# Recurrent mixer: the factors towards a chunk's end, made on ScalarE from those towards its beginning

## The chip, the cores and the metric

The kernel runs on one core of a Trainium2 chip, in one launch. The metric is device time in microseconds (us). The kernel before takes 2109.54 us, the median of three runs between 2107.28 and 2109.99.

## The reference, cut to what matters

The reference is a network of two layers over 512 tokens: 256 of context and 256 of the sequence proper. Each layer has a modulated norm, one input projection, three mixers side by side (neighbourhood attention with 8 heads, a recurrent mixer of the RWKV-7 kind with 4 heads of 64, and an mLSTM with 4 heads), an output projection, and a mixture of 32 experts of which each token takes two. The change is in the recurrent mixer alone:

```python
def rwkv7_scan(r, w, k, v, a, b, S0, emit):
    def step(S, inp):
        r_t, w_t, k_t, v_t, a_t, b_t = inp
        sa = jnp.einsum('bhvk,bhk->bhv', S, a_t)
        S = S * w_t[:, :, None, :] + sa[..., None] * b_t[:, :, None, :] + v_t[..., None] * k_t[:, :, None, :]
        return S, (jnp.einsum('bhvk,bhk->bhv', S, r_t) if emit else None)
...
    log_w = -jax.nn.softplus(-(w0 + jnp.einsum('blzr,zrc->blzc', wd, w2))) - 0.5
    decay = jnp.exp(-jnp.exp(log_w))
    a = jax.nn.sigmoid(a0 + jnp.einsum('blzr,zrc->blzc', ad, a2))
...
    k_dir = k[:, :, None] * (1.0 + (a - 1.0) * k_a)
    b_dir = kk.reshape(B, L, 1, RW_WIDTH) * a
```

It runs forward and backward (d = 0, 1). Since decay = exp(-kappa * s), with s a sigmoid and kappa = exp(-0.5), the product of decays over some steps is the exponential of a sum of s.

## The kernel before

Time is cut into 8 chunks of 64 steps, and the scan becomes products of small matrices: factors are applied to r, k, kk and b, so that what happens inside a chunk is matmuls, and only the state goes from chunk to chunk. The 256 columns are two halves (ct = 0, 1) of 128 partitions. So a layer has four items (d, ct), and a tile of 128x512 holds one item's 512 steps, each chunk 64 columns of it.

For each item `rw_feat` (line 645) makes the features. Two small matmuls and `sigm` (three activations) give S, the sigmoid s of the decay, and A, the a of the reference. A scan on VectorE (line 663) sums S inside each chunk: `cum`. From it come `tot` (the chunk's total), `Xx` = cum - S, and `Yy` = tot - cum. By direction these play three roles: `incl`, the sum up to a step with it; `excl`, the sum without it; `rem`, what remains to the chunk's end. ScalarE takes exponentials: `En` = exp(kappa * incl), and exp(-kappa * .) of incl, excl, rem and tot (`gc`). Then T gets -kk * excl and r * incl; `b` = kk * a; `kd` = k * (1 + (a - 1) * k_a), as a tensor_scalar on A and a product with k. BK holds b and kd times En: these stand in the matmuls inside the chunk (lines 697 to 704), whose masked results Aa go out to memory for the inverse (`rw_inv16`) and stay as MA. BH holds b and kd times rem: it is transposed (lines 717 to 721) and stands in the update of the state, in MA's first block. Line 725 copies a part of T over BK.

The two-tensor products go through the helper `tt` of line 649, so the profile shows them all on that line and tells them apart by tile: SA holds S and A, cX holds cum and Xx, and Yk holds Yy and kd. `CFG['fG']` chooses the engine of four of them. In layer 0 it is 0, and Xx, b and the two products of BH run on GpSimd; in layer 1 it is 1, and Xx runs on VectorE and the other three on GpSimd.

`rwkv` runs rw_feat of the next item, then `rw_mid`, `rw_inv16` of the next and `rw_seq` of this one. Beside them run the projections of the other mixers (`ml_proj`, `na_proj`), as filler for TensorE; their weights are split into a high and a low part, the high one on ScalarE (lines 472, 999), the low one on VectorE or GpSimd (lines 475, 1000). The program is written with a tile framework: a planner orders each engine's instructions by priority (offsets per function, in `CHOICES`) and by its own estimates of when operands are ready. Each engine then works in that fixed order and waits where an operand is late. BK and BH come from a pool of 15 pages, T, MA, Aa, SA, cX and Yk too.

After the mixers follow attention and mLSTM items with the output projection (`cores`), the routing, and the experts, whose weights stream from memory.

Of the kernel before, what the change touches and what calls it, by code (L numbers as in the profile page):

```python
# [14 lines left out]
AF = mybir.ActivationFunctionType  # L15
ALU = mybir.AluOpType
# [5 lines left out]
S = 256  # L22
# [5 lines left out]
KAPPA = float(np.exp(np.float32(-0.5)))  # L28
# [118 lines left out]
CFG = dict(CHOICES)  # L147
# [66 lines left out]
class K:  # L214
# [427 lines left out]
    def c8(self, t):  # L642
        return t.rearrange("p (c s) -> p c s", s=64)

    def rw_feat(self, d, ct, st):

        nc = self.nc
        V, G, A_ = nc.vector, nc.gpsimd, nc.scalar
        tt = lambda e, o, x, y, op: e.tensor_tensor(o, x, y, op)
        c8 = self.c8  # L650
        bc = lambda t: t.unsqueeze(2).to_broadcast([t.shape[0], t.shape[1], 64])
        sl = slice(ct * 512, (ct + 1) * 512)
        R, Kx, KK = self.Rf[:, sl], self.Kf[:, sl], self.KK[:, sl]
# [3 lines left out]
        S, A = self.w2("SA")  # L657
# [3 lines left out]
        self.sigm(A, ps, bias=self.nwa[:, 4 + j:5 + j], scale=-1.0)  # L661
        cum, Xx = self.w2("cX")
        V.tensor_tensor_scan(cum, self.rst, S, 0.0, ALU.mult, ALU.add)
        Yy, kd = self.w2("Yk")
        tot = self.sm([8], "tot")
        V.tensor_copy(tot, c8(cum)[:, :, 63])
        tt(V if CFG['fG'] & 1 else G, Xx, cum, S, ALU.subtract)
        tt(V, c8(Yy), bc(tot), c8(cum), ALU.subtract)
        if d == 0:
            incl, excl, rem = cum, Xx, Yy  # L670
        else:
            incl, excl, rem = S, Yy, Xx
            tt(V, S, S, Yy, ALU.add)
        T = st["T"] = self.w("T")
        tv = T.rearrange("p (c b s) -> p c b s", b=2, s=64)
        gc = st["gc"] = self.sm([8], f"gc{ct}", bufs=2)
# [2 lines left out]
        A_.activation(En, incl, AF.Exp, scale=KAPPA)  # L679
        A_.activation(excl, excl, AF.Exp, scale=-KAPPA)  # L680
        A_.activation(incl, incl, AF.Exp, scale=-KAPPA)
        A_.activation(rem, rem, AF.Exp, scale=-KAPPA)
        V.scalar_tensor_tensor(tv[:, :, 0, :], c8(KK), -1.0, c8(excl), ALU.mult, ALU.mult)
        tt(V, tv[:, :, 1, :], c8(R), c8(incl), ALU.mult)
        b = A
        V.tensor_scalar(kd, A, self.pr[:, 26 + ct:27 + ct], self.oka[:, ct:ct + 1], ALU.mult, ALU.add)
        tt(V if CFG['fG'] & 2 else G, b, KK, A, ALU.mult)
        tt(V, kd, kd, Kx, ALU.mult)
        BK, BH = self.w("BK"), self.w("BH")
        v4 = lambda t: t.rearrange("p (i b s) -> p i b s", b=4, s=64)  # L690
        i4 = lambda t: t.rearrange("p (i b s) -> p i b s", b=2, s=64)
        tt(V, v4(BK)[:, :, 0:4:3, :], i4(b), i4(En), ALU.mult)
        tt(V, v4(BK)[:, :, 1:3, :], i4(kd), i4(En), ALU.mult)
        tt(V if CFG['fG'] & 4 else G, v4(BH)[:, :, 0:4:3, :], i4(b), i4(rem), ALU.mult)
        tt(V if CFG['fG'] & 8 else G, v4(BH)[:, :, 1:3, :], i4(kd), i4(rem), ALU.mult)
        MA = st["MA"] = [self.w("MA"), self.w("MA")]
        Aa = st["Aa"] = self.w2("Aa")
        mk = self.c("maskA")[:, d * 128:(d + 1) * 128]
# [1 line left out]
        for g in range(2):  # L700
            pa = [self.pf(), self.pf()]
            for ci in range(4):
                c = g * 4 + ci
# [13 lines left out]
        for g in range(2):  # L717
            pt = self.pf()
            for ci in range(4):
                c = g * 4 + ci  # L720
# [12 lines left out]
        for pr in range(4):  # L733
            for hh in range(2):
                for par in range(2):
                    c = 2 * pr + par
# [1260 lines left out]
```

## Time and profile before

| | us |
|---|---|
| median of 3 runs | 2109.54 |
| profiled execution | 2105.22 |
| its span, first to last instruction | 2103.4 |
| TensorE busy (matmul) | 1835.3 |
| VectorE busy | 992.4 |
| ScalarE busy | 475.0 |
| GpSimd busy | 460.0 |

The profile is of one execution. Its slices show the recurrent mixer of layer 0 from about 95 to 350 us and that of layer 1 from about 1190 to 1440 us; from 600 to 1100 and from 1600 on the DMA engines are busy nearly all the time with expert weights. A busy time of TensorE says that matmuls were under way, not that it was at its peak. A wait is put down to the releaser that came last.

### The profile page before, as it was taken

What the parts mean: (1) busy time and instruction counts of PE and PEld (TensorE: products, weight loads), DVE (VectorE), ACT (ScalarE), POOL (GpSimd) and SP (SyncE); (2) the same over time, 40 slices, a digit from 0 to 9 for tenths busy, and PEclk for the clock granted to TensorE, in tenths of its full rate; (3) what the DMA queues carried; (4) which work ended last, traced back from release to release, by engine and by line L of the source; (5) the groups of instructions that cost most, each with busy time, mean ns of one, the idle gap of its engine ahead of it and who ended that gap; (6) DMA issues with size and microseconds to landing.
All of it is one profiled execution on the core that took longest, in us unless ns stands there. A gap on an engine that the chain in (4) does not pass through costs nothing. (4 is left out here: it accounts for less than half of the span.)

```text
span 2103.4 us, 29644 instructions
## 1 busy us (share of the span) xinstructions
PE 1835.3 (87%) x11375; PEld 952.4 (45%) x11379; DVE 992.4 (47%) x2079; ACT 475.0 (23%) x993; POOL 460.0 (22%) x338
## 2 busy tenths in 40 slices
PE   7989889989998899899995879899999888987985
PEld 3767666545443243224434667675443231323221
DVE  3687563467732334334447585653464122322223
ACT  2643222425210000000114542212331000000000
POOL 1232122234401112111125342231141001100001
PEclk9998999879999999999997888897799999999997
DMA  8332232751769998999992222244756969999995
GB/s 284 126 79 56 60 61 81 304 204 61 264 276 384 409 371 339 392 408 393 389 388 78 70 69 62 59 108 185 266 207 278 405 265 418 416 416 416 415 418 228
DMA packets 192881, 531.33 MB, mean 253 GB/s; under 512 B 77520, under 2 KB 107632, under 8 KB 155232
## 3 DMA queue, kind: packets, MB, share of 16 engines
q1 hardware_dynamic: 190656, 524.76, 65.9%
q0 software_dynamic: 928, 2.50, 0.4%
q8 instruction: 92, 1.51, 0.3%
q10 hardware_dynamic: 1152, 2.13, 0.3%
q14 instruction: 53, 0.43, 0.1%
HBM read 521.87 MB, written 7.47 MB: 252 GB/s over the span
## 5 line engine op out<-in xcount | busy, mean ns | idle before, releaser
L282 PE MATMUL ps<-rg,xe 128*32 128x512 f32 (+2 forms) x2280 | 484.2, 619 | 49.4 <-DMA rg<-in_exp_w_up_dram 29.8
L282 PE MATMUL pe<-rg,HT 128*32 128x512 f32 (+2 forms) x1120 | 233.8, 645 | 51.3 <-DMA rg<-in_exp_w_down_dram 41.0
L282 PE MATMUL ps<-rg,wh 128*128 128x512 f32 (+2 forms) x1056 | 263.4, 393 | 6.5 <-POOL wh L475 5.6
L282 PEld LDWEIGHTS ps<-rg,xe 128*32 128x32 f32 (+2 forms) x2280 | 109.3, 123 | 285.8 <-issue 180.7
L1666 POOL TENSOR_TENSOR acc<-acc,sc 128x512 f32<-128x512 f32 x82 | 106.1, 1293 | 585.5 <-DVE sc L1665 585.5
L1665 DVE TENSOR_TENSOR sc<-pw,bc 128x512 f32<-128x512 f32 x164 | 112.1, 690 | 230.0 <-PE pw L282 228.6
L282 PEld LDWEIGHTS ps<-rg,wh 128*128 128x128 f32 (+1 forms) x1056 | 183.6, 197 | 54.1 <-issue 13.0
L282 PEld LDWEIGHTS pe<-rg,HT 128*32 128x32 f32 (+2 forms) x1120 | 66.1, 130 | 214.2 <-issue 116.3
L1655 DVE SCALAR_TENSOR_TENSOR yl<-pe,sw,yh 128x512 fp32r<-128x512 f32 x54 | 40.4, 751 | 230.7 <-ACT yh L1654 227.9
L1654 ACT ACTIVATE yh<-pe,sw 128x512 fp32r<-128x512 f32 x54 | 36.9, 687 | 304.4 <-PE pe L282 281.4
L475 POOL TENSOR_TENSOR wh<-rg,wh 128x512 fp32r<-128x512 f32 (+1 forms) x44 | 60.7, 1386 | 182.7 <-ACT wh L472 182.2
L1601 POOL TENSOR_TENSOR ot<-m,m 128x512 fp32r<-128x512 f32 (+1 forms) x27 | 27.3, 1011 | 331.6 <-PE pw L286 285.3
L282 PE MATMUL pw<-oh,hi 128*128 128x256 f32 x336 | 89.9, 304 | 1.5 <-DVE oh L1569 1.5
L1631 ACT ACTIVATE H<-ps 128x512 f32<-128x512 f32 x27 | 16.1, 597 | 317.0 <-DVE acc L1666 300.6
L282 PE MATMUL pw<-yh,ot 128*128 128x512 f32 x164 | 85.2, 519 | 2.2 <-DVE sc L1665 1.9
L282 PE MATMUL ps<-wh,rg 128*128 128x256 f32 x384 | 83.2, 307 | 2.6 <-ACT VP L986 1.9
L282 PEld LDWEIGHTS pw<-yh,ot 128*128 128x128 f32 x164 | 31.0, 189 | 119.2 <-DVE sc L1665 57.6
L282 PE MATMUL pw<-oh,lo 128*128 128x256 f32 x336 | 82.8, 283 | 0.0
L282 PEld LDWEIGHTS pw<-oh,hi 128*128 128x128 f32 x336 | 64.1, 191 | 40.6 <-issue 24.9
L1603 DVE SCALAR_TENSOR_TENSOR m<-m,row 128x512 f32<-128x512 f32 (+1 forms) x54 | 28.3, 561 | 91.4 <-POOL ot L1601 91.4
L282 PEld LDWEIGHTS ps<-wh,rg 128*128 128x128 f32 x384 | 64.5, 202 | 10.4 <-issue 4.5
L282 PE MATMUL pw<-yl,ot 128*128 128x512 f32 x164 | 66.1, 403 | 0.7 <-DVE yl L1655 0.4
(432 smaller groups left out, 2850.7 us busy)
## 6 DMA issues: line engine op xcount, KB each, us to landing
rg<-in_exp_w_up_dram SPq DMA_DIRECT2D x127, 1024.0 KB, 11.7
rg<-in_exp_w_gate_dram SPq DMA_DIRECT2D x126, 1024.0 KB, 9.8
rg<-in_exp_w_down_dram SPq DMA_DIRECT2D x124, 1024.0 KB, 10.5
rg<-in_w_mod_dram SPq DMA_DIRECT2D x40, 1024.0 KB, 7.2
rg<-in_w_in_dram SPq DMA_DIRECT2D x26, 1024.0 KB, 5.7
rg<-in_w_mod_dram SPq DMA_DIRECT2D x16, 512.0 KB, 9.2
rg<-in_w_out_dram SPq DMA_DIRECT2D x8, 1024.0 KB, 8.2
bc<-modd SPq DMA_DIRECT2D x12, 512.0 KB, 4.1
```

Source lines behind the costliest of these rows:

```text
L282: return self.inorder(self.nc.tensor.matmul(out, lhsT, rhs, start=start, stop=stop, skip_group_check=True))
L475: eng.tensor_tensor(lo[:, :, d:d + w], t, hi[:, :, d:d + w], ALU.subtract)
L1601: nc.gpsimd.tensor_tensor(ot, m[0], m[1], ALU.add)
L1603: V.scalar_tensor_tensor(m[k], m[k], 1.0, self.wrow[k][:, :T], ALU.mult, ALU.mult, accum_out=sw[:, k:k + 1])
L1631: nc.scalar.activation(H, pgu[0][b], AF.Silu)
L1654: nc.scalar.activation(yh[:, sl], py[h2], AF.Copy, scale=sw)
L1655: V.scalar_tensor_tensor(yl[:, sl], py[h2], sw, yh[:, sl], ALU.mult, ALU.subtract)
L1665: V.tensor_tensor(tm, ps, self.g2b[0 if t >= 2 else 1][:, sl], ALU.mult)
L1666: (V if hf else nc.gpsimd).tensor_tensor(self.acc[t][:, sl], self.acc[t][:, sl], tm, ALU.add)
```

## The change

The remainder goes. A step's factor to the chunk's end is exp(-kappa * (tot - incl)) = exp(-kappa * tot) * exp(kappa * incl) = gc * En, so BH is BK times gc, chunk by chunk: eight activations (Copy with a column of gc as scale) of 128x128 on ScalarE. The exponential of `rem` and the two products of BH go. `kd`'s first step becomes an activation (Identity with scale and bias columns). `tot` is read in place from cum, without a copy. Direction 0 needs only Xx = cum - S, direction 1 only Xx = tot - cum; both run on VectorE, as does `b`, in both layers. `fG` is no longer read.

```diff
-        Yy, kd = self.w2("Yk")
-        tot = self.sm([8], "tot")
-        V.tensor_copy(tot, c8(cum)[:, :, 63])
-        tt(V if CFG['fG'] & 1 else G, Xx, cum, S, ALU.subtract)
-        tt(V, c8(Yy), bc(tot), c8(cum), ALU.subtract)
+        kd, b = self.w2("kb")
+        A_.activation(kd, A, AF.Identity, scale=self.pr[:, 26 + ct:27 + ct], bias=self.oka[:, ct:ct + 1])
+        tot = c8(cum)[:, :, 63]
         if d == 0:
-            incl, excl, rem = cum, Xx, Yy
+            incl, excl = cum, Xx
+            tt(V, Xx, cum, S, ALU.subtract)
         else:
-            incl, excl, rem = S, Yy, Xx
-            tt(V, S, S, Yy, ALU.add)
+            incl, excl = S, Xx
+            tt(V, c8(Xx), bc(tot), c8(cum), ALU.subtract)
+            tt(V, S, S, Xx, ALU.add)
...
-        A_.activation(rem, rem, AF.Exp, scale=-KAPPA)
...
-        b = A
-        V.tensor_scalar(kd, A, self.pr[:, 26 + ct:27 + ct], self.oka[:, ct:ct + 1], ALU.mult, ALU.add)
-        tt(V if CFG['fG'] & 2 else G, b, KK, A, ALU.mult)
+        tt(V, b, KK, A, ALU.mult)
...
-        tt(V if CFG['fG'] & 4 else G, v4(BH)[:, :, 0:4:3, :], i4(b), i4(rem), ALU.mult)
-        tt(V if CFG['fG'] & 8 else G, v4(BH)[:, :, 1:3, :], i4(kd), i4(rem), ALU.mult)
+
+        for c in range(8):
+            A_.activation(BH[:, c * 128:(c + 1) * 128], BK[:, c * 128:(c + 1) * 128], AF.Copy, scale=gc[:, c:c + 1])
```

## Rows read from the trace of the kernel before

**Rows 1.** Windows: us, busy (xcount) PE, PEld, DVE, ACT, POOL; PEclk, DMA, GB/s

```profile
97.00:350.00 253.00, 219.27 (x2248) 172.52 (x2247) 174.96 (x346) 81.08 (x158) 65.49 (x36) 0.92 0.25 57
1188.00:1440.00 252.00, 211.26 (x2199) 169.94 (x2197) 160.71 (x341) 77.73 (x158) 75.42 (x46) 0.88 0.32 83
```

**Rows 2.** Waits of PE, 97 to 350 us: total us, times, longest

```profile
PE pe L282 <- DVE BK L649: 19.1, 4, 6.4
...
PE ps L282 <- ACT VP L986: 1.9, 1, 1.9
```

**Rows 3.** Waits of PE, 1188 to 1440 us

```profile
PE pe L282 <- DVE BK L649: 17.5, 3, 8.6
...
PE ps L282 <- POOL wh L475: 5.6, 1, 5.6
```

**Rows 4.** Timeline, PE: start, us, what [idle before <-releaser]

```profile
109.25 2.08 PE L282 MATMUL pe<-T,BK 64*128 64x128 f32 x16 [6.41 <-DVE BK L649]
...
159.66 2.08 PE L282 MATMUL pe<-T,BK 64*128 64x128 f32 x16 [2.41 <-DVE BK L649]
...
215.64 2.08 PE L282 MATMUL pe<-T,BK 64*128 64x128 f32 x16 [5.38 <-DVE BK L649]
...
273.24 2.08 PE L282 MATMUL pe<-T,BK 64*128 64x128 f32 x16 [4.95 <-DVE BK L649]
...
1200.42 2.08 PE L282 MATMUL pe<-T,BK 64*128 64x128 f32 x16 [2.84 <-DVE BK L649]
...
1257.30 2.08 PE L282 MATMUL pe<-T,BK 64*128 64x128 f32 x16 [8.62 <-DVE BK L649]
...
1317.85 2.08 PE L282 MATMUL pe<-T,BK 64*128 64x128 f32 x16 [6.00 <-DVE BK L649]
```

**Rows 5.** Windows behind four waits, and one without a long wait

```profile
159.66:172.00 12.34, 12.34 (x74) 11.17 (x76) 10.60 (x17) 3.25 (x8) 1.39 (x1) 0.53 0.09 22
...
215.64:222.00 6.36, 6.36 (x42) 5.19 (x43) 3.25 (x9) 0.63 (x1) 0.00 (x0) 0.73 0.54 165
...
273.24:281.00 7.76, 7.76 (x50) 6.15 (x50) 3.29 (x9) 1.87 (x5) 0.00 (x0) 0.75 0.62 175
...
1364.27:1369.00 4.73, 4.73 (x12) 3.28 (x13) 3.85 (x3) 0.00 (x0) 4.73 (x3) 0.50 0.16 33
...
141.00:150.00 9.00, 7.09 (x52) 6.65 (x53) 8.50 (x9) 8.33 (x14) 4.93 (x2) 1.00 0.87 217
```

**Rows 6.** Timeline, items 0 of layer 0 and 3 of layer 1

```profile
97.84 1.23 DVE L663 TENSOR_TENSOR_SCAN cX<-rst,SA 128x512 f32<-128x512 bf16 x1 [1.06 <-ACT SA L549]
...
102.96 1.65 POOL L649 TENSOR_TENSOR SA<-rg,SA 128x512 f32<-128x512 f32 x1 [2.52 <-DVE Yk L686]
...
107.36 1.75 DVE L649 TENSOR_TENSOR BK<-Yk,SA 128x512 f32<-128x512 f32 x1
...
115.71 0.60 PE L286 MATMUL pe<-cst,BH 128*128 128x128 f32 x4
...
1357.87 4.68 POOL L649 TENSOR_TENSOR SA<-rg,SA 128x512 f32<-128x512 f32 x1 [11.11 <-DVE tot L666]
```

**Rows 7.** DVE products of the helper: ns least/median/greatest; and two alone

```profile
L649 DVE TENSOR_TENSOR Yk<-tot,cX x8: 684/1719/1784, 99.3 to 1358.3; 128x512 f32<-128x512 f32 x8
...
L649 DVE TENSOR_TENSOR Yk<-Yk,rg x8: 678/686/2852, 105.1 to 1358.9; 128x512 f32<-128x512 f32 x8
...
271.81 0.68 DVE L649 TENSOR_TENSOR BK<-SA,cX 128x512 f32<-128x512 f32 x1
...
272.41 0.68 DVE L649 TENSOR_TENSOR BK<-Yk,cX 128x512 f32<-128x512 f32 x1
```

**Rows 8.** ACT groups: total us, mean ns; idle before; wait in front of L725

```profile
L958 ACT ACTIVATE u<-ps,prm 128x512 f32<-128x512 f32 x6 | 4.6, 773 | 7.5 <-PE ps L282 7.5
...
L1124 ACT ACTIVATE Wp<-nd,uc 128x128 f32<-128x128 f32 x48 | 17.2, 390 | 1.7 <-DVE nd L1093 1.7
...
  ACT BK L725: 46.0, 7
```

## The prediction

> **What bounds the kernel now.** I read the busy time by windows first. The two stretches in which the recurrent mixer runs (layer 0 from 97 to 350 us, layer 1 from 1188 to 1440) hold TensorE busy for 219.27 of 253 us and 211.26 of 252, VectorE for 175 and 161, ScalarE for 81 and 78, the DMA engines for a quarter to a third [rows 1]. So TensorE sets the pace there, and what it does not work it waits: 33.7 us and 40.7 us. The list of who waited for whom comes next: the largest wait of TensorE in both stretches is for BK, 19.1 us in 4 waits and 17.5 us in 3 [rows 2, 3]. BK is the last product of rw_feat, the function that the diff edits. The other waits that the edit can reach are 1.9 us for VP and 5.6 us for a weight split on GpSimd [rows 2, 3]. The seven waits for BK follow one by one in the timeline [rows 4]. The matmuls after such a wait also run slower: the granted clock is 0.53 over the 12.34 us after the wait of item 1, and 0.73, 0.75 and 0.50 after three others (0.50 is the lower of the two levels, 1.2 GHz against 2.4); in 141 to 150 us, with 1.9 us of waits, it stays 1.00 [rows 5].
>
> A page's rule speaks against this reading. The Trainium skill (Trainium Kernel Development and Optimization, Performance Expectations) says that the matmul busy time is a poor measure of how near a kernel is to its limit, because matmuls are pipelined; by it TensorE's 0.86 would not prove that it paces the stretch, and a wait removed there could be given back. The trace can't show how full the pipe is, but in these waits nothing starts [rows 4], so I count the waits and not the busy share.
>
> **Why BK is late.** There are eight items (two layers, two directions, two column halves); item 0 of layer 0 stands for them [rows 6]. The scan ends at 99.07 and BK at 109.11: 10.0 us. Between stand seven VectorE products of 128x512, and one that runs beside a factor on GpSimd takes 1.75 us, where the same form alone takes 0.68 and the next starts 0.60 us after it [rows 6, 7]. Over all items the remainder Yk takes 684/1719/1784 ns (least, median, greatest) [rows 7]. So a GpSimd factor costs VectorE about 1.07 us for each product beside it, besides its own time (b: 1.65 us in item 0, 4.68 in item 3 of layer 1) [rows 6].
>
> **The change part by part.**
>
> VectorE. In direction 0 the copy of tot, Yk and kd go; b comes, and in layer 0 Xx comes from GpSimd. In direction 1 the copies of tot and kd go and b comes; Xx is now what Yk was. That leaves the scan and 7 products (direction 0) or 8 (direction 1). None of them now runs beside a factor on GpSimd. Scan end to BK end becomes: direction 0, Xx 0.60, then b and kd*K while ScalarE makes two exponentials, then T, T, BK, BK: 7 x 0.60 + 0.2 = 4.4 us. Direction 1: 8 x 0.60 + 0.1 = 4.9 us. To this I add what other steps have in VectorE's queue there now (0.3 to 1.4 us) and, where weight splits (L475, L1000) share GpSimd in those microseconds, 1.07 us for each product beside them: two products in items 2 and 3 of layer 0 (2.1 us), one beside a rope step in item 0 of layer 1, four or so (4.8 us, since rows go up to 2852 ns) beside the 5.6 us split in item 2 of layer 1 [rows 7].
>
> The eight terms, each read the same way (scan end to BK end before, after, what TensorE recovers of its wait in rows 4). Layer 0: item 0 10.0 to 5.8, recovers 4.2 of 6.41; item 1 9.3 to 5.1, 4.2 of 1.94 + 2.41 (the VP wait goes too: its ScalarE copy queues behind an exponential that waited for Yk); item 2 11.8 to 7.7, 4.2 of 5.38; item 3 11.9 to 8.3, 3.6 of 4.95. Layer 1: item 0 7.9 to 5.8, 2.1 of 2.84; item 1 8.8 to 5.1, 3.7 of 8.62; item 2 13.1 to 9.7, 3.4 of 6.00; item 3: the wait is for a weight split that stands behind b in GpSimd's queue (b ran from 1357.87 to 1362.55) [rows 6]; with b gone the split starts some 4.6 us sooner, 4.6 of 5.62. Sum: 30.0 us.
>
> TensorE's clock. Where less than those 1.9 us remain of a wait, I let the slow stretch behind it go: 12.34 x 0.47 = 5.8 (item 1), 6.36 x 0.27 = 1.7 (item 2), 7.76 x 0.25 = 1.9 (item 3), 4.73 x 0.50 = 2.4 (the split) [rows 5]: 11.8 us. The other four keep theirs: 2.2, 4.9 and 2.6 us remain of three, and in front of item 0 of layer 1 a wait for u stays. Together 41.8 us.
>
> ScalarE. The exponential of rem goes; I count nothing for it. kd comes: an Identity with scale and bias columns, 0.77 us in rows 8, while ScalarE waits for the scan anyway. The eight scalings of 128x128 by a column have the shape of L1124: 0.39 us each [rows 8], 8 x 0.39 = 3.1 us at most, less where they overlap, nothing at least. I take 3.1 and put it beside TensorE's work: ScalarE sat idle for 46.0 us in 7 waits in front of the copy of L725, which is the next thing behind BK in its queue [rows 8]. BH is first needed by the transposes, which start 6.4 us after the first matmul on BK (115.71 against 109.25) [rows 6]. If that cover is gone, the cost is 3.1 us in each of eight items, 25 us.
>
> The Trainium skill (ScalarE: Activation LUTs, Rules for kernel authors) says the opposite of this edit: multiplications and additions belong on VectorE and not on ScalarE. By it the scalings would be two VectorE products, 1.2 us by rows 7, and the sum would not be better: on VectorE they would stand in the queue that is late, on ScalarE they fill a wait [rows 8]. So I don't follow it here.
>
> GpSimd. Three or four products per item go; nothing else is behind them but splits and rope steps, which come sooner (the 4.6 us above). No DMA is issued in the edited lines; the write of Aa (SP's queue) and the load of its inverse follow the matmuls on BK by the same steps as now, so they come sooner with them. After the mixer the stages are not bound to a fixed time: whatever ends sooner shifts them.
>
> What is given back. Order on each queue is set by the framework's planner from its own estimates, so an edit of about ten instructions in eight places rearranges both stretches. TensorE's other waits there (for T, PV, u and so on) are 74.4 - 36.6 - 7.5 = 30.3 us in [rows 1 to 3]. The trace of before can't show the new order; bounds are -10 (some of these waits go too) and +42 (all is lost again). I take 14, about half of the other waits, as an estimate. **Forecast: 41.8 - 14 = 28 us less.** The profiled execution took 2105.22 us (span 2103.4), so 2077; the median of the runs shown is 4.3 us above it, so 2081 us.
>
> **The rivals.**
> - All of it comes, and little is given back: 42 to 50 us less, 2060 to 2068. For it: every stretch behind the mixer merely shifts. Against: four waits keep a rest of 0.7 to 4.9 us. Chance 0.18.
> - The wait moves with the work: BK is due sooner, so the planner puts its matmuls sooner, and TensorE waits as long, with the filler behind. Then only the split and VP gain: 7.5 us at most, some 2104. For it: today's order is no better than that. Against: the waits are as long as what GpSimd adds to VectorE, which is what would go. Chance 0.12.
> - VectorE stays slow, because the splits left on GpSimd move beside the products in all items: half of the 30.0 comes, no clock with it, and half of the 14 is given back: 8 us less, 2101. For it: those splits are in every stretch. Against: in four items none stands there now. Chance 0.08.
> - Slower: ScalarE becomes the gate. It works in order; the eight scalings wait for BK, and behind them stand the weight casts (L472) that feed TensorE's filler and the copy of L725. If the matmuls on BK also move forward (rival two), TensorE meets the transposes before BH is ready. Price: 3.1 us at most in eight items, 25, less the 7.5 and part of the 3.1 hidden: +10 to +20, 2120 to 2130. It decides where the transposes stand less than 3.1 us behind the first matmul on BK. Today they stand 6.4 us behind. Chance 0.15.
> - My forecast, 14 to 36 us less (2073 to 2095): chance 0.47.
>
> **How the numbers follow.** 2081 is the forecast; its own range is 2073 to 2095. For 8 in 10 the range goes down into the first rival (2060) and up over the second and third to 2112; outside lie most of the slower case (0.13) and 0.07 below. A measurement of this kernel can tell about 0.2% (4.2 us) from no change. Faster by more than that: 0.47 + 0.18 + 0.08 + a quarter of 0.12 = 0.76; within it 0.09; slower 0.15.
>
> **What would show it.** VectorE's products of rw_feat at 0.68 us where no split is beside them; TensorE's wait for BK at 10 us or less in all (36.6 now); a granted clock above 0.92 and 0.88 in the two stretches; the eight scalings inside ScalarE's wait, with no wait of TensorE for BH. I am wrong if the wait for BK stays above 25 us, if waits for BH, T or PV grow by what it lost, or if the stages after the mixer take longer than now.

## The result, and the profile after

The kernel after takes 2055.31 us (median of 4 runs, 2050.79 to 2062.86), the kernel before, beside it, 2109.76 (2107.28 to 2118.54): ratio 0.975, interval 0.971 to 0.979. That is 54 us less, where 28 were forecast, and below the range. The profiled execution took 2055.75 us with a span of 2054.0, so it lost 49.5 of the 2105.22 us of the one before. One run of e6_layer0, an experiment below, took 2789 us at a granted clock of 0.55 and is left out of that kernel's median and ratio.

Where the time went is read best from windows cut at the same instructions in both kernels: from the first lora matmul of a layer's mixer to the first reduction of its head norm (the mixer), and from there to MAX8, the router's instruction on its scores (the first one in layer 0, the last one in layer 1). First the kernel before, then the kernel after; columns as in [rows 1].

```profile
91.92:352.00 260.08, 226.27 (x2280) 177.16 (x2280) 176.38 (x348) 86.07 (x166) 67.38 (x37) 0.92 0.25 58
352.00:563.10 211.10, 194.81 (x979) 106.96 (x982) 129.98 (x269) 84.50 (x224) 77.72 (x47) 0.87 0.53 196
1185.94:1443.40 257.46, 215.22 (x2216) 171.44 (x2215) 162.97 (x346) 79.71 (x162) 76.45 (x47) 0.88 0.32 86
1443.40:1576.90 133.50, 124.78 (x576) 66.45 (x578) 70.69 (x166) 51.49 (x138) 40.03 (x33) 0.80 0.59 217
```

```profile
91.92:332.00 240.08, 218.88 (x2270) 171.06 (x2270) 156.43 (x344) 96.30 (x198) 41.31 (x21) 0.96 0.27 61
332.00:539.90 207.90, 190.90 (x988) 103.83 (x992) 129.91 (x270) 84.38 (x224) 78.10 (x46) 0.90 0.55 202
1166.64:1396.20 229.56, 201.85 (x2184) 162.97 (x2183) 147.15 (x338) 89.76 (x194) 50.56 (x35) 0.93 0.34 85
1396.20:1524.30 128.10, 117.10 (x612) 64.58 (x610) 72.40 (x166) 51.91 (x138) 39.61 (x33) 0.87 0.67 246
```

The mixers lost 20.0 and 27.9 us. A window less TensorE's busy time is its idle time: 33.8 to 21.2 us in layer 0, 42.2 to 27.7 in layer 1, 27.1 us less together. The other 20.8 us are busy time (7.4 and 13.4) of about the same matmuls. That part is the clock: busy time times granted clock stays put (226.27 x 0.92 = 208, 218.88 x 0.96 = 210; 215.22 x 0.88 = 189, 201.85 x 0.93 = 188). What follows the mixers lost 3.2 and 5.4 us, idle a little up, clock from 0.87 to 0.90 and from 0.80 to 0.87. So 56.5 us left these stages; everything else (routers, experts, the projections between the layers) took 7.0 us more than before, 49.5 in all.

TensorE's waits in the two mixers, the answer to [rows 2, 3], first layer 0, then layer 1:

```profile
PE pe L282 <- DVE BK L649: 4.1, 3, 2.8
PE pw L282 <- DVE PV L811: 4.1, 3, 3.5
PE pw L282 <- DVE T L860: 3.7, 1, 3.7
```

```profile
PE pe L282 <- DVE BK L649: 8.8, 1, 8.8
PE ps L282 <- DVE u L963: 5.5, 1, 5.5
PE pw L282 <- ACT T L825: 4.0, 1, 4.0
PE ps L282 <- POOL wh L475: 1.2, 2, 0.7
```

BK, VP and the weight split wh together fell from 44.1 us [rows 2, 3] to 14.1: 30.0. All other waits rose from 31.9 to 34.8. No row in either mixer names BH. The waits for BK that are left, in the timeline (the answer to [rows 4]):

```profile
105.65 1.16 PE L282 MATMUL pe<-T,BK 64*128 64x128 f32 x16 [2.81 <-DVE BK L649]
...
151.69 1.16 PE L282 MATMUL pe<-T,BK 64*128 64x128 f32 x16 [0.44 <-DVE BK L649]
...
203.38 1.16 PE L282 MATMUL pe<-T,BK 64*128 64x128 f32 x16 [0.90 <-DVE BK L649]
...
1178.12 2.08 PE L282 MATMUL pe<-T,BK 64*128 64x128 f32 x16 [8.77 <-DVE BK L649]
```

The sixteen matmuls behind the first three take 1.16 us, where all seven of before took 2.08 [rows 4]. The last, item 0 of layer 1, still takes 2.08, behind a longer wait than before. In the kernel before, TensorE waited there for u first and for BK after it (2.84 us, [rows 4]):

```profile
1195.08 1.22 PE L282 MATMUL ps<-u,cst 128*128 128x256 f32 x2 [6.43 <-DVE u L965]
```

Now the matmuls on u stand behind those on BK, and one wait of 8.77 us has taken the place of two with 9.27. So the split hangs on the name that a wait is given: with this wait for u counted beside the one for BK, 36.4 us went and the others rose by 9.3. The sum of both, 27.1 us, does not hang on it.

The windows of the first and the last group show the clock, 1.00 and 0.50, under the same number of matmuls:

```profile
105.65:106.81 1.16, 1.16 (x17) 1.04 (x17) 1.16 (x3) 1.16 (x5) 0.00 (x0) 1.00 0.00 0
...
1178.12:1180.20 2.08, 2.08 (x17) 1.85 (x17) 1.07 (x3) 2.08 (x8) 0.73 (x1) 0.50 0.00 0
```

Item 0 of layer 0, the answer to [rows 6]: scan, products, ScalarE's scalings, first matmuls on BK, transposes of BH.

```profile
97.85 1.23 DVE L663 TENSOR_TENSOR_SCAN cX<-rst,SA 128x512 f32<-128x512 bf16 x1 [1.06 <-ACT SA L549]
...
99.11 0.69 DVE L649 TENSOR_TENSOR cX<-cX,SA 128x512 f32<-128x512 f32 x1
...
101.16 0.68 DVE L649 TENSOR_TENSOR kb<-rg,SA 128x512 f32<-128x512 f32 x1
...
104.82 0.68 DVE L649 TENSOR_TENSOR BK<-kb,SA 128x512 f32<-128x512 f32 x1
...
105.54 2.45 ACT L693 ACTIVATE BH<-BK,gc 128x128 f32<-128x128 f32 x8 [0.35 <-DVE BK L649]
...
110.17 0.63 PE L286 MATMUL pe<-cst,BH 128*128 128x128 f32 x4
```

From the scan's end (99.08) to BK's end (105.50) it is 6.4 us, where it was 10.0; forecast 5.8. The scalings end at 107.99, 2.2 us ahead of the transposes. Over all items, the products (the answer to [rows 7]) and ScalarE's new steps ([rows 8]):

```profile
L649 DVE TENSOR_TENSOR BK<-kb,SA x8: 682/685/686, 102.4 to 1223.7; 128x512 f32<-128x512 f32 x8
L649 DVE TENSOR_TENSOR BK<-kb,cX x8: 677/680/1770, 202.0 to 1319.8; 128x512 f32<-128x512 f32 x8
L649 DVE TENSOR_TENSOR cX<-cX,SA x4: 682/689/2899, 99.1 to 1220.0; 128x512 f32<-128x512 f32 x4
```

```profile
L693 ACT ACTIVATE BH<-BK,gc 128x128 f32<-128x128 f32 x64 | 19.6, 388 | 7.4 <-DVE BK L649 7.4
L665 ACT ACTIVATE kb<-SA,drv,prm 128x512 f32<-128x512 f32 x8 | 6.5, 813 | 0.1
```

### The profile page after: what moved, and what is told of

It reads as the page before. It is cut to its first block, busy times and chain, and to the rows that moved or that the text cites. A ratio compares the mean times of both kernels' runs of the same rounds, so it can differ in the third digit from the quotient of the medians.

```text
span 2054.0 us, 29667 instructions
## 1 busy us (share of the span) xinstructions
PE 1812.5 (88%) x11375; PEld 934.3 (45%) x11379; DVE 958.0 (47%) x2067; ACT 495.5 (24%) x1057; POOL 407.9 (20%) x310
## 5 line engine op out<-in xcount | busy, mean ns | idle before, releaser
L282 PE MATMUL pe<-rg,HT 128*32 128x512 f32 (+2 forms) x1120 | 241.5, 662 | 52.8 <-DMA rg<-in_exp_w_down_dram 41.3
L282 PE MATMUL ps<-rg,wh 128*128 128x512 f32 (+2 forms) x1056 | 258.6, 388 | 4.4 <-ACT wh L472 1.5
L1629 ACT ACTIVATE H<-ps 128x512 f32<-128x512 f32 x27 | 16.1, 597 | 318.6 <-DVE acc L1664 308.3
```

The lines of the kernel that those rows point to most:

```text
L282: return self.inorder(self.nc.tensor.matmul(out, lhsT, rhs, start=start, stop=stop, skip_group_check=True))
L1629: nc.scalar.activation(H, pgu[0][b], AF.Silu)
```

## The experiments

Theory 1 (T1): BK came late because GpSimd's factors ran beside VectorE's products and because of the steps that the change drops from VectorE's queue; TensorE waited for it and ran at a lower clock behind the wait. The rivals: the planner's new order alone made the difference, the new place of BH did, or one layer's gain hangs on the other. The table holds every kernel that ran. Stages: span's start to layer 0's first MAX8 of the router, and layer 1's first lora matmul to its last MAX8, of the one profiled execution; idle, busy and the wait for BK are TensorE's, the first two in those stages together.

| kernel | layer 0 | layer 1 | idle | busy | wait for BK | median us | ratio to before |
|---|---|---|---|---|---|---|---|
| before | 563.1 | 391.0 | 117.3 | 836.8 | 36.6 | 2109.8 | |
| after | 539.9 | 357.7 | 93.5 | 804.0 | 12.9 | 2055.3 | 0.975 (0.971 to 0.979) |
| e3_pool_beside | 550.4 | 367.7 | 108.3 | 809.8 | 23.0 | 2069.1 | 0.982 (0.978 to 0.986) |
| e11_pool_full | 560.0 | 379.5 | 114.7 | 824.9 | 25.5 | 2078.0 | 0.984 (0.979 to 0.989) |
| e1_all_vector | 552.8 | 364.5 | 101.1 | 816.2 | 18.4 | 2068.1 | 0.980 (0.977 to 0.983) |
| e2_b_pool | 538.3 | 360.8 | 90.7 | 808.4 | 16.4 | 2043.8 | 0.968 (0.964 to 0.972) |
| e4_bh_vector | 539.9 | 372.0 | 98.4 | 813.5 | 17.4 | 2057.3 | 0.976 (0.973 to 0.980) |
| e5_bh_pool | 548.7 | 357.7 | 93.8 | 812.6 | 13.3 | 2053.2 | 0.971 (0.967 to 0.975) |
| e10_kd_vector | 540.3 | 364.6 | 96.0 | 808.9 | 17.1 | 2045.9 | 0.973 (0.969 to 0.976) |
| p_before_mid | 568.9 | 393.1 | 118.2 | 843.8 | 37.3 | 2103.1 | 1.000 (0.997 to 1.002) |
| p_after_mid | 542.8 | 358.0 | 93.3 | 807.5 | 14.0 | 2047.8 | 0.972 (0.969 to 0.976) |
| e6_layer0 | 538.9 | 391.3 | 107.8 | 822.5 | 22.3 | 2082.4 | 0.989 (0.985 to 0.993) |
| e7_layer1 | 561.7 | 356.8 | 106.6 | 811.9 | 28.0 | 2066.8 | 0.984 (0.980 to 0.987) |
| c1_mid_bpool | 541.3 | 358.0 | 96.4 | 802.9 | 16.1 | 2041.6 | 0.970 (0.966 to 0.973) |

The kernels ran in three groups, each beside the kernel before on its own chip (2111.65, 2105.28 and 2103.97 us), so ratios are compared, not times. What lies outside the stages of the table (span less their sum) is 1140 to 1149 us in the profiled executions of all other kernels and 1156 in that of the kernel after, and a profiled execution need not lie at its kernel's median (e10's took 2055.73): the stages show the cause, the ratios the size.

**e3_pool_beside: idle GpSimd products put back beside VectorE.** In the kernel after:

```
+        self.scr = cp.tile([P, 256], F32, name="scr")
...
+        for x in (b, kd):
+            for h in range(2):
+                tt(G, self.scr, x[:, 256 * h:256 * h + 256], En[:, 256 * h:256 * h + 256], ALU.mult)
```

Nobody reads the scratch tile. In the traces the order of instructions on TensorE, VectorE and ScalarE is that of the kernel after, instruction for instruction.

> The changed kernel with four GpSimd products of 128x256 added per item (b and kd times En, into a scratch tile that nobody reads), so the order of TensorE's, VectorE's and ScalarE's instructions stays exactly that of the changed kernel. Theory 1 (a GpSimd product slows the VectorE products beside it, and that made BK late): two to three products of rw_feat per item go from 0.68 towards 1.75 us, BK is 2 to 3 us later in eight items, the waits for BK and the half clock behind them come back: 2075 to 2090 us. Theory 2 (fewer steps in the chain are the gain, contention is incidental) and theory 3 (the gain is the planner's new order): 2052 to 2060, as the changed kernel.

Measured: 2069.13 us, ratio 0.982. The stages are 20.5 us longer, 14.8 in TensorE's idle time and 5.7 in its busy time. Its products of the helper:

```profile
L650 POOL TENSOR_TENSOR scr<-kb,SA x16: 719/1051/1108, 101.4 to 1230.6; 128x256 f32<-128x256 f32 x16
...
L650 DVE TENSOR_TENSOR BK<-kb,SA x8: 677/1204/1228, 101.8 to 1231.0; 128x512 f32<-128x512 f32 x8
...
L650 DVE TENSOR_TENSOR BK<-kb,cX x8: 1204/1212/1224, 209.1 to 1332.6; 128x512 f32<-128x512 f32 x8
```

The very products that take 0.68 us in the kernel after take 1.2 beside GpSimd's, in the same order of instructions, and the wait for BK grows by 10.1 us. This shows the contention, with the order of these three engines unchanged, and its price: 20.5 us of stage time, with 10.1 us more of that wait. A part of the price lies in GpSimd's own queue, which is longer too: TensorE's wait for its weight split wh (1.2 us in the kernel after) is 3.6. The time lies below T1's range and above that of its rivals; by the ratio, whose interval just meets that of the kernel after, a little over a quarter of the gain is lost.

**e11_pool_full: the same, and idle GpSimd products in the place of b and Xx.**

```
+        for _ in range(2 - self.l):
+            for h in range(2):
+                tt(G, self.scr, KK[:, 256 * h:256 * h + 256], A[:, 256 * h:256 * h + 256], ALU.mult)
```

> As e3_pool_beside, and in addition the GpSimd work of b and (in layer 0) Xx as products of KK and A into the scratch tile that nobody reads, from where A is ready: GpSimd does about the work of the kernel before, in the new algebra. VectorE's and ScalarE's order is exactly that of the changed kernel, TensorE's nearly. Theory 1 (GpSimd beside VectorE): more than half of the gain of the changed kernel is lost, 2080 to 2100 us. Theory 2 (the dropped steps) and 3 (the order): the gain stays but for the 15 us that e3_pool_beside lost, 2062 to 2075.

Measured: 2077.99 us, ratio 0.984; the stages are 41.9 us longer than after's, of 56.5 that the change took. The mixers, cut as above, are about as long as those of the kernel before (261.0 and 250.2 us; 260.1 and 257.5 before, 240.1 and 229.6 after), with about its clock:

```profile
92.30:353.30 261.00, 230.40 (x2270) 179.49 (x2270) 169.12 (x345) 96.46 (x199) 75.87 (x53) 0.91 0.24 56
1183.96:1434.20 250.24, 214.51 (x2184) 174.11 (x2183) 158.88 (x339) 89.89 (x194) 75.49 (x59) 0.86 0.30 78
```

But this profiled execution is the slowest of the four (2089.09 us; the others took 2063 to 2078). By its ratio e11 lies by e3 (the intervals overlap), under T1's range and above that of its rivals, and has lost a little over a third of the gain, where T1 expected more than half. So GpSimd beside VectorE is shown as a cause, and how much of the gain it is stays open between a third and three quarters.

**e1_all_vector: the old algebra with every factor on VectorE.** In the kernel before:

```
- 'L': [{'fG': 0,
+ 'L': [{'fG': 15,
...
-        'fG': 1,
+        'fG': 15,
```

> The kernel before with all factors on VectorE in both layers (fG = 15), the old algebra kept (Yk, rem, tot, kd on VectorE, two BH products on VectorE behind BK). Theory 1: no factor on GpSimd, so the products take 0.68 us; Yk, tot and kd still stand in the chain (about 1.2 us an item) and BH delays VectorE behind it by 1.2: 55 to 75 in a hundred of the gain, 2070 to 2080 us. Theory 2 (the dropped steps are the gain): 2105 to 2115, since VectorE only gets more work. Theory 3: anything, some 15 us around 2105.

Measured: 2068.09 us, ratio 0.980: four fifths of the gain (T1 had 55 to 75 in a hundred), by moving work onto the engine whose queue was late. In direction 0 the products of BK all take 0.68 us, though BH's two now stand in the same queue; in direction 1 two of the second ones are still slow, where a weight split (L1000) runs on GpSimd beside them:

```profile
L649 DVE TENSOR_TENSOR BK<-SA x4: 677/684/687, 104.4 to 1234.3; 128x512 f32<-128x512 f32 x4
L649 DVE TENSOR_TENSOR BK<-Yk,SA x4: 679/682/686, 105.0 to 1234.9; 128x512 f32<-128x512 f32 x4
...
L649 DVE TENSOR_TENSOR BK<-Yk,cX x4: 679/1776/2869, 211.9 to 1333.4; 128x512 f32<-128x512 f32 x4
```

What is left for the new algebra (no Yk, no exponential of rem, kd and BH on ScalarE) is 0.980 to 0.975, whose intervals overlap, so the ratios don't show it; by the stages of the profiled executions it is 19.7 us.

**e2_b_pool: the kernel after with b on GpSimd.**

```
-        tt(V, b, KK, A, ALU.mult)
+        tt(G, b, KK, A, ALU.mult)
```

> The changed kernel with b alone back on GpSimd in both layers. Theory 1: b takes 1.7 us or more instead of 0.68 and slows one or two VectorE products beside it: BK 1 to 3 us later per item, 2065 to 2080 us. Theory 2: VectorE has a step less, 2050 to 2058. Theory 3: no relation, some 15 us around 2065.

Measured: 2043.81 us, ratio 0.968. T1 as I had put it missed: b takes 1284 to 1749 ns there, and BK in direction 1 takes 1.75 us (median) beside it, but TensorE's wait for BK grows by 3.5 us only, its idle time falls by 2.8, and the stages are as long as after's (899.1 and 897.6). The time is below that of all three theories. So one slow product per item does not show in the time, and e3's four do. That other work covers it is not shown: unlike in e3, the order of instructions on TensorE, VectorE and ScalarE is not that of the kernel after, and what this order gained or lost is in the same numbers.

**e5_bh_pool and e4_bh_vector: BH in two products, on GpSimd (e5) or on VectorE (e4).**

```
-        for c in range(8):
-            A_.activation(BH[:, c * 128:(c + 1) * 128], BK[:, c * 128:(c + 1) * 128], AF.Copy, scale=gc[:, c:c + 1])
+        for h in range(2):
+            tt(G, c16(BH)[:, 4 * h:4 * h + 4], c16(BK)[:, 4 * h:4 * h + 4], gc[:, 4 * h:4 * h + 4].unsqueeze(2).to_broadcast([P, 4, 128]), ALU.mult)
```

e4 has V for G.

> The changed kernel with BH = BK times gc made by two GpSimd products instead of eight ScalarE scalings. They start only when BK is done, so no product in the chain to BK runs beside them. Theory 1: BK is as early as in the changed kernel, and only BH comes some 1 us later: 2053 to 2066 us. A rival by which any GpSimd factor costs, wherever it stands: 2070 to 2085.

> The changed kernel with BH = BK times gc made by two VectorE products of 128x512 instead of eight ScalarE scalings, as the Trainium skill (ScalarE: Activation LUTs, Rules for kernel authors) would have it. My reading: VectorE is the queue that is late, so 1.2 us more in it per item cost 4 to 12 us: 2058 to 2068. By the rule: no worse than the changed kernel, 2050 to 2056.

Measured: 2053.18 and 2057.3 us, ratios 0.971 and 0.976. By the ratios the place of BH makes no difference that can be told, so ScalarE's eight scalings cost nothing that shows. By the stages they are the best place: layer 0 of e5 is 8.8 us longer than that of the kernel after, layer 1 of e4 14.3. The whole executions (2054.7 and 2056.8 us, 2055.75 for the kernel after) are as long only because the kernel after has 10 and 13 us more outside the stages. Which of the two tells the price is open. In e5 BH stands behind BK, and BK's products stay at 0.68 us (median) with GpSimd at work. The Trainium skill (ScalarE: Activation LUTs, Rules for kernel authors), which wants multiplications on VectorE, changes nothing here by the ratio: 0.976 with them there, 0.975 with them on ScalarE.

**e10_kd_vector: kd's affine step back on VectorE.**

```
-        A_.activation(kd, A, AF.Identity, scale=self.pr[:, 26 + ct:27 + ct], bias=self.oka[:, ct:ct + 1])
+        V.tensor_scalar(kd, A, self.pr[:, 26 + ct:27 + ct], self.oka[:, ct:ct + 1], ALU.mult, ALU.add)
```

> The changed kernel with kd's affine step (A times a column plus a column) back on VectorE, so one more 128x512 step in VectorE's queue in each of eight items. Theory 1 (every step in VectorE's chain between scan and BK is paid by TensorE, and the runs so far show 2 to 2.3 us of stage time for 1 us of wait for BK): 8 x 0.68 = 5.4 us of chain, 5 to 12 us slower than the changed kernel, 2060 to 2067. Rival (kd falls into the time in which VectorE waits for the exponentials anyway): no more than 3 us, 2052 to 2058.

Measured: 2045.94 us, ratio 0.973, against 0.975 for the kernel after: by which T1 missed. The wait for BK grew by 4.2 us and the stages of the profiled execution, the slowest of six, by 7.3, as T1 had it, but the ratio shows nothing of it. So neither side is shown. With e2 it says that T1 can't be read step by step: a single step more in the chain, in another order of instructions, does not show in the ratio.

**p_before_mid and p_after_mid: another order by the planner.** In both kernels and both layers:

```
-        'pr': {'rw_mid': -200,
+        'pr': {'rw_mid': -150,
```

> The kernel before with the planner's offset of rw_mid changed from -200 to -150 in both layers: another order, the same work. Theory 1: the waits for BK stay, within 10 us of the kernel before: 2100 to 2120. Theory 3 (order decides): 20 us or more off, either way.

> The changed kernel with the same change of offset. Theory 1: within 10 us of the changed kernel: 2045 to 2065, so that the difference to p_before_mid is again 45 to 60 us. Theory 3: the difference between the two is below 30 us or above 75.

Measured: 2103.13 and 2047.83 us on the same chip, 55.3 us apart, with 2105.28 for the kernel before. With another order in both kernels the change is worth the same, so one lucky order is not its cause.

**e6_layer0 and e7_layer1: the change in one layer.** The old and the new rw_feat side by side, chosen by the layer:

```
+        return (self.rw_feat_new if self.l == 0 else self.rw_feat_old)(d, ct, st)
```

e7 has `self.l == 1`.

> The change in layer 0 alone; layer 1 has the old rw_feat. Theory 1 (every item gains by itself: what GpSimd and the dropped steps added to VectorE's chain, and TensorE's clock with it): layer 0 up to its first MAX8 of the router falls from 563 to 540 us (535 to 545), layer 1's from its first lora matmul to its last MAX8 stays at 391 (386 to 396); 23 us less in all, 2086 (2081 to 2091). Rival (the gain of one layer hangs on the other, by the planner's order over the whole program or by what the clock carries over): less than 12 or more than 40 us less, 2098 and up or 2070 and down, and the two single layers do not add to the 54 of the whole change.

> The change in layer 1 alone. Theory 1: layer 0 stays at 563 us (558 to 568), layer 1 falls from 391 to 358 (353 to 363), 33 us less in all: 2076 (2071 to 2082); with the run of layer 0 alone the two gains add to 50 to 60. Rival: they add to less than 40 or more than 70.

Measured: ratios 0.989 and 0.984, so 1.1% and 1.6%, which add to 2.7% where the whole change has 2.5%. The medians are 2082.4 us, in T1's range, and 2066.8, under it, beside a kernel before of 2103.97. The stages, e6 first, then e7 (columns as in [rows 1]):

```profile
0.00:538.90 538.90, 482.28 (x3576) 319.39 (x3580) 323.09 (x706) 215.47 (x487) 141.31 (x99) 0.95 0.45 146
1158.96:1550.30 391.34, 340.17 (x2793) 238.10 (x2793) 236.34 (x512) 131.13 (x300) 114.62 (x80) 0.85 0.41 131
```

```profile
0.00:561.70 561.70, 495.50 (x3576) 328.01 (x3580) 345.15 (x710) 205.47 (x455) 167.24 (x115) 0.92 0.43 139
1183.53:1540.30 356.77, 316.40 (x2792) 223.57 (x2792) 219.10 (x503) 141.74 (x332) 90.12 (x68) 0.91 0.46 143
```

Each layer with the change is as long as in the kernel after, each without it as long as before, within 2 us. The clock goes with it: 0.95 and 0.85 in e6, 0.92 and 0.91 in e7. So nothing that one layer gains is taken back in the other, and the clock is a matter of the layer's own waits and order.

**c1_mid_bpool: e2 and p_after_mid together**, the two that ran a little under the kernel after.

> The changed kernel with b = KK*A on GpSimd and the planner's offset of rw_mid at -150 instead of -200 in both layers: the two variants that ran a little under the changed kernel, together. Theory 1 (neither touches the mixers' length: b alone on GpSimd ran with the same stages, 899 against 898 us; what they gained lies in the expert stages, whose length moves by 5 us from run to run of the same code): 2040 to 2056, about 2046. Rival (both are real gains and add): 2036 or less.

Measured: 2041.64 us, ratio 0.970, with stages of 899.3 us. It is the lowest median, but not the lowest ratio (e2), its interval overlaps that of the kernel after, and the stages are no shorter; no version here is shown to beat the change.

## Why the prediction was wrong in size

The mechanism was right and the direction too. The forecast was 30.0 (eight chain terms) + 11.8 (clock) - 14 (given back) = 27.8; measured in the profiled executions 30.0 - 2.9 + 20.8 + 8.6 (behind the mixers) - 7.0 (the other stages) = 49.5.

**The step that failed is "What is given back. ... I take 14, about half of the other waits".** Only 2.9 us came back: TensorE's other waits in the mixers went from 31.9 to 34.8 us. (Or 9.3, with the wait for u counted as said above; what the edit reached is then 36.4 instead of 30.0, and together they miss by the same.) The argument was that an edit in eight places rearranges both stretches. It does, but no row said that the new order would be worse: with another order in both kernels the change is worth the same (55 us), and the layers add. This term is 11.1 us of the miss.

**The clock term was mis-sized: 11.8 forecast, 20.8 measured** (7.4 in layer 0, where 9.4 were counted, 13.4 in layer 1, where 2.4 were). I let go only the slow stretches behind waits of which little should remain, and kept those behind the others. In layer 1 the waits of items 1 and 2 went entirely, where I had kept 4.9 and 2.6 us, and their stretches with them. The row of the kernel before that I should have read and did not, the 12 us behind the wait of 8.62 us (a granted clock at the lower level, with TensorE busy throughout, so 6 us of full-clock work lost):

```profile
1257.30:1269.30 12.00, 12.00 (x63) 10.71 (x64) 7.01 (x15) 2.41 (x5) 0.56 (x1) 0.50 0.38 111
```

In the kernel after, the one long wait that is left has such a stretch, and item 1 has none. In layer 0 the stretch of item 1, for which 5.8 us were counted, is still partly slow (third row), with a wait of 1.78 us for MA in it that the kernel before doesn't have:

```profile
1176.00:1186.00 10.00, 7.88 (x39) 6.44 (x40) 7.87 (x19) 5.96 (x16) 5.01 (x6) 0.50 0.18 52
...
1225.51:1237.51 12.00, 11.40 (x139) 8.94 (x138) 11.65 (x20) 6.40 (x16) 2.83 (x2) 1.00 0.16 31
...
151.69:164.03 12.34, 10.56 (x89) 9.79 (x91) 9.77 (x18) 5.66 (x17) 0.00 (x0) 0.72 0.09 23
```

**"Whatever ends sooner shifts them" was not the whole.** The stages behind the mixers took 8.6 us less, all of it busy time at a higher clock (11.6 us less busy, idle up by 3.0). Layer 0's 3.2 us do not hang on the change in that layer: cut the same way, e7, which has the old rw_feat there, takes 207.8 us behind the mixer (211.1 before, 207.9 after). In layer 1 it is 134.3 us without the change (e6) and 130.6 with it (e7; 133.5 before, 128.1 after). By what these gains come was not tried and is open. The 7.0 us more in the other stages are open too: outside the stages of the table the kernel after has 1156 us and no other kernel has more than 1149, but that execution (2055.75 us) lies at the kernel's median, so it need not be an odd one.

**The eight chain terms: right as a sum, by luck.** 30.0 us forecast, 30.0 measured for BK, VP and wh. Layer 0 follows the terms: 2.81, 0.44, 0.90 and 0 us remain (2.2, 0.15, 1.2 and 1.35 by the prediction). In layer 1 the waits of items 1 and 2 went entirely instead of in part, 7.5 us more than forecast, and that of item 0 grew from 2.84 to 8.77, where 0.7 should remain, since the matmuls on u moved behind it: 8.0 us less. That the two cancel is luck. Nor does BK's own lateness give each wait. In the kernel after, scan and BK of item 1, first in layer 0, then in layer 1:

```profile
141.93 1.23 DVE L663 TENSOR_TENSOR_SCAN cX<-rst,SA 128x512 f32<-128x512 bf16 x1 [0.75 <-ACT SA L549]
...
150.34 1.29 DVE L649 TENSOR_TENSOR BK<-kb,SA 128x512 f32<-128x512 f32 x2
...
1218.27 1.22 DVE L663 TENSOR_TENSOR_SCAN cX<-rst,SA 128x512 f32<-128x512 bf16 x1
...
1223.11 1.29 DVE L649 TENSOR_TENSOR BK<-kb,SA 128x512 f32<-128x512 f32 x2
```

From the scan's end to BK's end it is 8.5 us in layer 0 (9.3 before, 5.1 forecast), only 0.8 less, and the waits of that item fell by 3.9; in layer 1 it is 4.9 (8.8 before, 5.1 forecast), 3.9 less, and a wait of 8.62 went. There the new order of TensorE's other work took part; how much of the 30.0 us it is, is not shown.

**VectorE's price beside GpSimd: right.** 0.68 us alone in the kernel after; 1.2 us beside the idle products of e3. But it is not a price that TensorE always pays (e2), nor one that VectorE always pays. In item 0 of layer 1 of the kernel before, b runs on GpSimd for 4.40 us, four VectorE products beside it keep 0.68 (first and last below), and it is GpSimd's that is long:

```profile
1192.97 4.40 POOL L649 TENSOR_TENSOR SA<-rg,SA 128x512 f32<-128x512 f32 x1 [21.67 <-DVE tot L666]
...
1193.41 0.68 DVE L649 TENSOR_TENSOR Yk<-tot,cX 128x512 f32<-128x512 f32 x1
...
1195.55 0.68 DVE L649 TENSOR_TENSOR T<-rg,cX 128x512 f32<-128x512 f32 x1
```

**ScalarE: right.** The eight scalings take 2.45 us as a group (3.1 at most forecast), kd 0.81 (0.77 forecast); TensorE has no wait for BH. The slower rival, ScalarE as the gate, needed the transposes less than 3.1 us behind the first matmul on BK; in item 0 of layer 0 they stand 4.5 us behind (110.17 against 105.65).

**TensorE as the pace-setter: right.** By the Trainium skill (Trainium Kernel Development and Optimization, Performance Expectations) a high busy share would not prove it. Here 27.1 of the 30.0 us of waits removed are gone from TensorE's idle time, so it did set the pace. (Its busy share is 0.87 and 0.84 by [rows 1], where the prediction has 0.86.)

Of the signs named in advance all but one came: the wait for BK ended at 12.9 us instead of 10 or less, for item 0 of layer 1. The rival closest to what happened is "all of it comes", and even that was too small, because it had the clock at 11.8.

## What to carry to other kernels

Before you subtract "something is given back", look for the wait that would take it; here 30.0 us of waits went and 2.9 came back. Where the granted clock is at its lower level behind a wait, count the whole stretch until it rises, for every wait that may go, not only for those that surely go: in this kernel TensorE got back 27.1 us of idle time in the mixers and 20.8 of clock. And a helper engine can lengthen the queue that it is to shorten: all factors from GpSimd back on the late VectorE gave four fifths of the gain, while a single step moved (b, kd, BH) can't be told from nothing by the ratio.

## What the runs showed of the hardware

- A VectorE product of two 128x512 float32 operands takes 0.68 us alone, 1.20 to 1.23 beside GpSimd products of 128x256 in e3, about 1.75 beside one of 128x512 ([rows 6], and BK in direction 1 of e2). TensorE did not always pay for it: 20.5 us of stage time in e3, 1.5 in e2, whose order is another.
- In item 0 of layer 0 of the kernel before, a slowed product ends 0.55 us behind the end of the GpSimd product that was under way when it started: 105.16 behind 104.61 (b, [rows 6]), 109.11 behind 108.55 (below; BK in [rows 6]). In item 0 of layer 1 VectorE's products kept 0.68 us and b on GpSimd took 4.40. So which of the two is slowed differs from place to place.

```profile
103.40 1.76 DVE L649 TENSOR_TENSOR T<-rg,cX 128x512 f32<-128x512 f32 x1
...
106.91 1.64 POOL L649 TENSOR_TENSOR BH<-Yk 128x512 f32<-128x512 f32 x1 [0.63 <-DVE Yk L649]
```

- Granted clock at the lower level outlasts the wait: 12 us after the wait of 8.62 us it had not risen, with TensorE busy all the time.
- Sixteen small matmuls (64x128 on T and BK) take 1.16 us at a granted clock of 1.00 and 2.08 at 0.50. Behind a wait of 2.81 us in item 0 of layer 0 of the kernel after they ran at 1.00, behind one of 2.41 in the kernel before, which had another of 1.94 just ahead of it, at 0.50 (2.08 us, [rows 4]): the length of the last wait alone does not say which.
